# A two-block transformer on one core: routing, gate and memory-norm steps held in program order, bias rows repeated by transfers

## The chip, the cores and the metric

The kernel runs on one core of one Trainium2 chip. The metric is device time in microseconds (us), the median of repeated executions. Lower is better. The engines that matter here are TensorE (PE, matrix products), VectorE (DVE), ScalarE (ACT), GpSimd (POOL, here only an issuer of transfers) and SyncE (SP, the issuer of weight loads). Each takes its instructions strictly in the order in which they stand in its queue: one that waits holds up everything behind it on that engine.

## The reference, cut to what matters

256 tokens of width 2048 go through two blocks. The change touches the second half of the first block (`peer`) and the preparation of a bias for the second.

```python
def peer(h, wq, k1, k2, u, v):
    t = h.reshape(-1, d)                                # 256 x 2048
    q = (t @ wq).reshape(T, 8, 2, 128)
    s1 = jnp.einsum('thd,hnd->thn', q[:, :, 0], k1)     # 128 scores per head and half
    s2 = jnp.einsum('thd,hnd->thn', q[:, :, 1], k2)
    v1, i1 = lax.top_k(s1, 16)
    v2, i2 = lax.top_k(s2, 16)
    cand = v1[..., :, None] + v2[..., None, :]          # 16 x 16 candidates
    sc, pos = lax.top_k(cand, 16)                       # the 16 experts of a token and head
    g = jax.nn.softmax(sc, axis=-1)
    act = gelu(u[idx] @ t);  out = sum(g * act * v[idx])  # over 16384 experts
...
dist_bias = rel_bias[t5_bucket(jnp.arange(S))].T        # 8 heads, one bias per distance
m = rmsnorm_2(mem, g_mem)                               # needs the sums of squares of mem
```

## The kernel before

**The work.** Nearly all of it is dense matrix products in float32, each done as three products of a high and a low part: activations are split into `hTh` and `hTl`, and each block of weights into `whi` and `wlo`. The experts are not gathered: all 16384 rows of `u` are multiplied (`up`, eight groups of 2048 experts), the result is multiplied by a gate that is zero for experts not chosen (`gate`), and then by all rows of `v` (`down`, eight groups).

**The weight stream.** `load_w` brings 1 MB of weights into one of three `raw` buffers through SP's queue. `split_w` (two calls per `raw`) makes `whi` with a cast on ACT (line 114) and `wlo` with a subtraction on DVE (line 115, which needs `whi`). There are three buffers of each, so the two engines can be at most three splits ahead of PE. In `gemm_block` (down, and most projections) one split feeds 12 products of 512 columns (line 147), in `gemm_cols` (up) 24 products of 256 columns (lines 174 to 176).

**Side work.** Everything else is written as Python generators that are put in a queue (`later`). `step(rate)`, called after each 1 MB of weights, traces the next pieces of them, each up to its next `yield`. The rates stand in `RATES`: 1.5 pieces per MB in the last projection before `up` and in the first three groups of `up`, 0.6 in `down`, 1.7 in the third group of `down`. `drain()` traces what is left.

**The order.** The queue of an engine is not the order of tracing. A scheduler sorts the instructions of each engine by its own estimate of when their inputs are ready, and so it can move a traced instruction ahead of others on its engine if no data stand against it.

**The pieces that the change touches.**
- `route` (lines 799 to 838), 16 times: for one head and half of the tokens, the top 16 of two sets of 128 scores (`top16`), the sums of the pairs, the top 16 of those, the two indices (lines 818 to 829), then the softmax (an Exp on ACT at line 836). It is all on DVE except for small casts and the Exp on ACT. Five pieces each.
- `all_gates`: one-hot rows for 8 tokens at a time on DVE (`ohA`, `ohB`), products on PE, and the gates written to DRAM (`gd`).
- `gate(e)`: for each of four pieces, the activations and gates are fetched from DRAM into one of three `ag` buffers (`fetch`, POOL's queue), multiplied on DVE (line 955), cast to `hTh` on ACT (line 958) and subtracted to `hTl` on DVE (line 959). It prepares `down(e)` during `down(e-1)`, and `gate(0)` during the last group of `up`.
- `ahead`, during the third group of `down`: the memory (2 MB) is brought into two `raw` buffers of the weight stream and squared and summed on ACT (`sq_sum`, line 251, tile `ssm`); then one row of biases per head is computed by a matrix product (line 996), repeated on all 128 partitions, copied (line 998) and written to DRAM (`bd`), from where the second block reads it.

Of the kernel before, what the change touches and what calls it, by code (L numbers as in the profile page):

```python
# [9 lines left out]
F32 = mybir.dt.float32  # L10
# [3 lines left out]
AF = mybir.ActivationFunctionType  # L14
OP = mybir.AluOpType
# [4 lines left out]
P = 128  # L20
# [35 lines left out]
def build(tc, A, out):  # L56
    nc = tc.nc
    mm = nc.tensor.matmul

    es = ExitStack()  # L60
    with es:
# [40 lines left out]
        def drain():  # L102
            flush(-1)
            step(-1)

# [143 lines left out]
        def sq_sum(x, acc_col, n=512):  # L249
            junk = main.tile([P, 512], F16, name="junk", bufs=1)  # L250
            nc.scalar.activation(junk[:, :n], x, AF.Square, accum_out=acc_col)
# [10 lines left out]
        env = dict(locals())  # L262
# [485 lines left out]
def peer(env):  # L748
    z = NS(env)
    nc, ps, main, wp, A, tc, mm = z.nc, z.ps, z.main, z.wp, z.A, z.tc, z.mm  # L750
# [5 lines left out]
    with phase_pool(tc, "peer") as pp:  # L756
# [31 lines left out]
        def top16(src, vals, idx):  # L788
            n = src.shape[-1]
            tmp = scr[:, 3, 0:T]  # L790
            nc.vector.max(vals[:, 0:8], src)
# [5 lines left out]
        def route(h, t):  # L797
# [3 lines left out]
            for j in range(2):  # L801
# [5 lines left out]
            nc.vector.tensor_add(  # L807
                cd,
                v[:, 0].unsqueeze(2).to_broadcast([P, 16, 16]),
                v[:, 1].unsqueeze(1).to_broadcast([P, 16, 16]),  # L810
# [7 lines left out]
            nc.vector.tensor_scalar(ab[:, 0], pu, 4, None, OP.logical_shift_right)  # L818
# [16 lines left out]
            nc.vector.tensor_scalar_mul(mx, sc[:, 0:1], -1.0)  # L835
# [34 lines left out]
        def all_gates():  # L870
# [4 lines left out]
            for t0 in range(0, T, TG):  # L875
                gs = pp.tile([P, P, TG], F32, name="gs", bufs=3)
                for tb in range(0, TG, 8):
# [6 lines left out]
                    nc.vector.tensor_tensor(four(B2), io, row(i2T, t), OP.is_equal)  # L884
# [59 lines left out]
        def gate(e):  # L944
# [5 lines left out]
            for nb in range(4):  # L950
# [4 lines left out]
                nc.vector.tensor_mul(av, av, g.rearrange("p b c t -> p c b t"))  # L955
                yield
                cs = slice(nb * 4, nb * 4 + 4)
                nc.scalar.copy(wh[:, cs], a)  # L958
# [18 lines left out]
        def ahead():  # L977

            ssm = main.tile([P, 2, 4], F32, name="ssm", bufs=1)
            for t in range(2):  # L980
                mn = z.load_w(A["mem"][:, t].rearrange("p (a b) -> p a b", b=512))
                for b in range(4):
                    z.sq_sum(mn[:, b], ssm[:, t, b : b + 1])
                    yield
# [6 lines left out]
            nc.gpsimd.dma_start(bk, A["bucket"])  # L991
            env["bd"] = z.dram.tile([8, P, 384], F32, name="bd")
            yield
            for h in range(8):
                pb = z.mm_tile()
                mm(pb[:, :384], rb[:, h : h + 1].to_broadcast([33, P]), bk, start=True, stop=True)
                bv = pp.tile([P, 384], F32, name="bv", bufs=2)
                nc.scalar.copy(bv, pb[:, :384])
                nc.gpsimd.dma_start(env["bd"][h], bv)
                yield  # L1000
# [492 lines left out]
```

## Time and profile before

| | us |
|---|---|
| median of three executions | 3224.32 (3224.06 to 3224.76) |
| the profiled execution's own time | 3223.47 |
| its span, first to last instruction | 3221.7 |
| PE busy | 3183.3 |
| DVE busy | 2004.5 |
| ACT busy | 1529.6 |

The span is 1.8 us shorter than the time of the same execution. Busy is the time in which an engine had an instruction running; products follow each other in a pipeline, so a busy PE is one that was never left without work, not one at its peak.

### The profile page before, as it was taken

To read this page: it belongs to the slowest core of one execution; us is meant where nothing else is said; L and a number is where in the kernel's file an instruction comes from. 1 tells how busy PE (TensorE), PEld (TensorE's weight loads), DVE (VectorE), ACT (ScalarE), POOL (GpSimd) and SP (SyncE) were. 2 spreads that over 40 slices of the span, in tenths; PEclk is the share of its full clock that TensorE was granted. 3 is DMA by queue.
4 is the path that set the end of the run, shared out by engine and by line. 5 is a ranking of instruction groups with operands and counts; after the bars stand their busy time and mean duration, and the time that the engine had idled before them with its cause. 6 is when DMAs were issued, how large, how long until landed. Compare 5 with 4: busy or idle time off the path is not lost.

```text
span 3221.7 us, 45786 instructions
## 1 busy us (share of the span) xinstructions
PE 3183.3 (99%) x18818; PEld 2766.7 (86%) x18818; DVE 2004.5 (62%) x2812; ACT 1529.6 (47%) x1967; POOL 92.2 (3%) x126
## 2 busy tenths in 40 slices
PE   8999999999999999999999999999999999999998
PEld 7877788999999999777787778888888989899897
DVE  6665679955666654555555555799666555555555
ACT  6456555544444444444443444545656434444344
POOL 0000000000000010000100000000000000000000
PEclk9999999999999999999999999999999999999999
DMA  6544454565667786667666765555554555555554
GB/s 234 183 144 171 144 180 157 200 209 203 229 240 248 242 289 214 233 235 239 231 223 228 240 215 183 196 183 177 176 170 170 185 189 189 183 186 189 187 183 157
DMA packets 101475, 647.31 MB, mean 201 GB/s; under 512 B 11269, under 2 KB 12421, under 8 KB 32400
## 3 DMA queue, kind: packets, MB, share of 16 engines
q1 hardware_dynamic: 82512, 575.63, 51.7%
q0 software_dynamic: 18752, 68.74, 6.4%
q8 instruction: 147, 2.41, 0.3%
q14 instruction: 64, 0.52, 0.0%
HBM read 607.11 MB, written 37.22 MB: 200 GB/s over the span
## 4 chain that ended last, share of the span: by engine, by line
PE 72%; issue 15%; DVE 6%; DMA 4%; POOL 1%; ACT 1%; SPq 0%; ACTq 0%; POOLq 0%; DVEq 0%
PE acc L147 52%; PE acc L176 5%; PE acc L174 5%; PE acc L175 5%; DMA ag<-gd 3%; DVE wlo L115 2%; PE tp L214 1%; DVE scr L793 0%; POOL gd L898 0%; DVE i L828 0%; PE mm L743 0%; DVE hTl L959 0%; DMA raw<-in_peer_v_dram 0%; DMA raw<-in_mem_dram 0%; POOL act L915 0%
## 5 line engine op out<-in xcount | busy, mean ns | idle before, releaser
L115 DVE TENSOR_TENSOR wlo<-raw,whi 128x1024 fp32r<-128x1024 f32 x1064 | 1300.1, 1223 | 1041.8 <-ACT whi L114 1038.1
L114 ACT CAST whi<-raw 128x1024 fp32r<-128x1024 f32 x1064 | 1114.6, 1049 | 1455.2 <-PE acc L147 853.0
L147 PE MATMUL acc<-whi,hTh 128*128 128x512 f32 x2650 | 1061.7, 401 | 10.5 <-ACT whi L114 10.5
L147 PE MATMUL acc<-wlo,hTh 128*128 128x512 f32 x2650 | 1051.5, 397 | 7.0 <-DVE wlo L115 6.8
L147 PE MATMUL acc<-whi,hTl 128*128 128x512 f32 x2650 | 1050.8, 397 | 0.0
L176 PE MATMUL acc<-hTh,wlo 128*128 128x256 f32 x3072 | 866.8, 282 | 10.1 <-DVE wlo L115 9.9
L174 PE MATMUL acc<-hTh,whi 128*128 128x256 f32 x3072 | 868.0, 283 | 0.0
L175 PE MATMUL acc<-hTl,whi 128*128 128x256 f32 x3072 | 863.6, 281 | 0.0
L147 PEld LDWEIGHTS acc<-whi,hTh 128*128 128x128 f32 x2650 | 498.7, 188 | 132.7 <-ACT whi L114 10.9
L147 PEld LDWEIGHTS acc<-wlo,hTh 128*128 128x128 f32 x2650 | 499.0, 188 | 129.0 <-DVE wlo L115 13.2
L147 PEld LDWEIGHTS acc<-whi,hTl 128*128 128x128 f32 x2650 | 498.4, 188 | 120.7 <-issue 0.3
L176 PEld LDWEIGHTS acc<-hTh,wlo 128*128 128x128 f32 x3072 | 579.4, 189 | 14.9 <-DVE wlo L115 14.4
L174 PEld LDWEIGHTS acc<-hTh,whi 128*128 128x128 f32 x3072 | 579.8, 189 | 0.2
L175 PEld LDWEIGHTS acc<-hTl,whi 128*128 128x128 f32 x3072 | 579.7, 189 | 0.2
L1087 DVE SCALAR_TENSOR_TENSOR cc<-hc,vec,cc 128x256 f32<-128x256 f32 x240 | 102.1, 478 | 0.5
L955 DVE TENSOR_TENSOR ag<-ag 128x1024 f32<-128x1024 f32 x32 | 39.2, 1225 | 61.5 <-DMA ag<-gd 61.2
L958 ACT CAST hTh<-ag 128x1024 fp32r<-128x1024 f32 x32 | 32.9, 1050 | 31.7 <-DVE ag L955 22.5
L675 DVE TENSOR_TENSOR x<-acc,x 128x512 f32<-128x512 f32 x72 | 46.4, 681 | 0.3 <-PE acc L147 0.2
L911 DVE TENSOR_TENSOR at<-acc,rtok 128x512 f32<-128x512 f32 x64 | 43.7, 690 | 0.5
L959 DVE TENSOR_TENSOR hTl<-ag,hTh 128x1024 fp32r<-128x1024 f32 x32 | 38.5, 1222 | 1.6 <-ACT hTh L958 0.8
L915 POOL DMA_DIRECT2D act<-at x32 | 17.4, 545 | 741.4 <-ACT at L913 741.1
L940 POOL DMA_DIRECT2D ag<-gd x32 | 37.4, 1170 | 6.3 <-DMA gd<-gs 5.1
(314 smaller groups left out, 1496.3 us busy)
## 6 DMA issues: line engine op xcount, KB each, us to landing
raw<-in_peer_u_dram SPq DMA_DIRECT2D x128, 1024.0 KB, 4.9
raw<-in_peer_v_dram SPq DMA_DIRECT2D x128, 1024.0 KB, 4.9
raw<-in_w_dram SPq DMA_DIRECT2D x128, 1024.0 KB, 4.9
raw<-in_w_in_dram SPq DMA_DIRECT2D x83, 1024.0 KB, 4.9
raw<-in_w_out_dram SPq DMA_DIRECT2D x32, 1024.0 KB, 4.9
raw<-in_wq_dram SPq DMA_DIRECT2D x16, 1024.0 KB, 4.9
act<-at POOLq DMA_DIRECT2D x32, 512.0 KB, 4.3
gd<-gs POOLq DMA_DIRECT2D x16, 1024.0 KB, 5.6
```

What stands on the lines that cost most here:

```text
L114: nc.scalar.copy(hi[:, :kt, :n], raw[:, k0 : k0 + kt, :n])
L115: nc.vector.tensor_sub(lo[:, :kt, :n], raw[:, k0 : k0 + kt, :n], hi[:, :kt, :n].bitcast(F32))
L147: mm(o, a, b, start=start, stop=stop)
L174: mm(o, hi[:, k, cs], xh[:, kk], start=kk == 0 and c % 2 == 0, stop=False)
L175: mm(o, hi[:, k, cs], xl[:, kk], start=False, stop=False)
L176: mm(o, lo[:, k, cs], xh[:, kk], start=False, stop=kk == 15 and c % 2 == 1)
L675: nc.vector.tensor_add(x[:, t, sl], acc[t], x[:, t, sl])
L911: nc.vector.tensor_mul(at[:, 2 * c : 2 * c + 2], acc[c], rt)
L940: nc.gpsimd.dma_start(g, gd[e, :, :, nb * 4 : nb * 4 + 4])
L955: nc.vector.tensor_mul(av, av, g.rearrange("p b c t -> p c b t"))
L959: nc.vector.tensor_sub(wl[:, cs], a, wh[:, cs].bitcast(F32))
L1087: nc.vector.scalar_tensor_tensor(o, hc[:, c, tap : tap + T], w[:, tap : tap + 1], o, OP.mult, OP.add)
```

## The change

`pin` puts an instruction behind the last one that was traced before it on its own engine. It adds no wait at run time; it only takes from the scheduler the freedom to move that instruction forward. What depends on a pinned instruction moves with it. Pinned are: the first `max` of each `top16`, the sums of pairs, the first index step and the first softmax step in `route`; the first comparison of each group of 8 tokens in `all_gates`; the product (line 955) and the cast (line 958) in `gate`; each `sq_sum` of the memory in `ahead`, which is now also traced two pieces after its load; and the one product of the biases. That product makes all 8 heads at once, without repetition. Its 8 rows go to DRAM (`bd1`), are read back repeated on 128 partitions, four heads at a time (`br`, in the buffers of `at`), and are written to `bd`.

```diff
@@ -102,6 +102,9 @@
         def drain():
             flush(-1)
             step(-1)
+
+
+        pin = tc.keep_in_program_order
 
         def load_w(src, kt=4, n=512):
             raw = wp.tile([P, 4, 512], F32, name="raw", bufs=3)
@@ -248,7 +251,7 @@
 
         def sq_sum(x, acc_col, n=512):
             junk = main.tile([P, 512], F16, name="junk", bufs=1)
-            nc.scalar.activation(junk[:, :n], x, AF.Square, accum_out=acc_col)
+            return nc.scalar.activation(junk[:, :n], x, AF.Square, accum_out=acc_col)
 
 
         con = const.tile([P, NCON], F32)
@@ -788,7 +791,7 @@
         def top16(src, vals, idx):
             n = src.shape[-1]
             tmp = scr[:, 3, 0:T]
-            nc.vector.max(vals[:, 0:8], src)
+            z.pin(nc.vector.max(vals[:, 0:8], src))
             nc.vector.max_index(idx[:, 0:8], vals[:, 0:8], src)
             nc.vector.match_replace(tmp[:, :n], vals[:, 0:8], src, -3e38)
             nc.vector.max(vals[:, 8:16], tmp[:, :n])
@@ -804,10 +807,12 @@
             fi = rp.tile([P, 2, 16, 16], F16, name="if_p", bufs=1)
             nc.scalar.copy(fi, iu.unsqueeze(3).to_broadcast([P, 2, 16, 16]))
             cd = scr[:, 3, T : 2 * T].rearrange("p (a b) -> p a b", b=16)
-            nc.vector.tensor_add(
-                cd,
-                v[:, 0].unsqueeze(2).to_broadcast([P, 16, 16]),
-                v[:, 1].unsqueeze(1).to_broadcast([P, 16, 16]),
+            z.pin(
+                nc.vector.tensor_add(
+                    cd,
+                    v[:, 0].unsqueeze(2).to_broadcast([P, 16, 16]),
+                    v[:, 1].unsqueeze(1).to_broadcast([P, 16, 16]),
+                )
             )
             sc = rp.tile([P, 16], F32, name="sc_p", bufs=2)
             pu = rp.tile([P, 16], U32, name="pu_p", bufs=2)
@@ -815,7 +820,7 @@
             top16(cd.rearrange("p a b -> p (a b)"), sc, pu)
             yield
             ab = rp.tile([P, 2, 16], U32, name="ab_p", bufs=2)
-            nc.vector.tensor_scalar(ab[:, 0], pu, 4, None, OP.logical_shift_right)
+            z.pin(nc.vector.tensor_scalar(ab[:, 0], pu, 4, None, OP.logical_shift_right))
             nc.vector.tensor_scalar(ab[:, 1], pu, 15, None, OP.bitwise_and)
             abf = rp.tile([P, 2, 16], F16, name="abf_p", bufs=2)
             nc.scalar.copy(abf, ab)
@@ -832,7 +837,7 @@
 
             mx = rp.tile([P, 1], F32, name="mx_p", bufs=2)
             sm = rp.tile([P, 1], F32, name="sm_p", bufs=2)
-            nc.vector.tensor_scalar_mul(mx, sc[:, 0:1], -1.0)
+            z.pin(nc.vector.tensor_scalar_mul(mx, sc[:, 0:1], -1.0))
             nc.scalar.activation(sc, sc, AF.Exp, bias=mx, accum_out=sm)
             nc.vector.reciprocal(sm, sm)
             nc.scalar.mul(gsel[:, t, h * 16 : h * 16 + 16], sc, sm)
@@ -881,7 +886,7 @@
                     A1 = pp.tile([P, 8, P], F16, name="ohA", bufs=1)
                     B2 = pp.tile([P, 8, P], F16, name="ohB", bufs=2)
                     Ag = [pp.tile([P, 8, P], F16, name="ohA%d" % k, bufs=2) for k in range(2)]
-                    nc.vector.tensor_tensor(four(B2), io, row(i2T, t), OP.is_equal)
+                    z.pin(nc.vector.tensor_tensor(four(B2), io, row(i2T, t), OP.is_equal))
                     nc.vector.tensor_tensor(four(A1), io, row(i1T, t), OP.is_equal)
                     yield
                     for k, g in enumerate((gh, gl)):
@@ -952,10 +957,10 @@
                 a = ag[:, 0].rearrange("p (c t) -> p c t", c=4)
                 g = ag[:, 1].rearrange("p (b c t) -> p b c t", c=4, t=TG)
                 av = a.rearrange("p c (b t) -> p c b t", t=TG)
-                nc.vector.tensor_mul(av, av, g.rearrange("p b c t -> p c b t"))
+                z.pin(nc.vector.tensor_mul(av, av, g.rearrange("p b c t -> p c b t")))
                 yield
                 cs = slice(nb * 4, nb * 4 + 4)
-                nc.scalar.copy(wh[:, cs], a)
+                z.pin(nc.scalar.copy(wh[:, cs], a))
                 nc.vector.tensor_sub(wl[:, cs], a, wh[:, cs].bitcast(F32))
                 fetch()
                 yield
@@ -979,8 +984,10 @@
             ssm = main.tile([P, 2, 4], F32, name="ssm", bufs=1)
             for t in range(2):
                 mn = z.load_w(A["mem"][:, t].rearrange("p (a b) -> p a b", b=512))
+                yield
+                yield
                 for b in range(4):
-                    z.sq_sum(mn[:, b], ssm[:, t, b : b + 1])
+                    z.pin(z.sq_sum(mn[:, b], ssm[:, t, b : b + 1]))
                     yield
             env["rm"] = z.rstd_of(ssm, D, "rstdm")
 
@@ -989,14 +996,19 @@
             nc.vector.memset(rb[32:33], NEG)
             nc.gpsimd.dma_start(rb[0:32], A["rel_bias"])
             nc.gpsimd.dma_start(bk, A["bucket"])
+            bv = pp.tile([8, 384], F32)
+            yield
+            pb = z.mm_tile()
+            z.pin(mm(pb[:8, :384], rb, bk, start=True, stop=True))
+            nc.scalar.copy(bv, pb[:8, :384])
+            bd1 = z.dram.tile([8, 384], F32, name="bd1")
+            nc.gpsimd.dma_start(bd1, bv)
+
             env["bd"] = z.dram.tile([8, P, 384], F32, name="bd")
-            yield
-            for h in range(8):
-                pb = z.mm_tile()
-                mm(pb[:, :384], rb[:, h : h + 1].to_broadcast([33, P]), bk, start=True, stop=True)
-                bv = pp.tile([P, 384], F32, name="bv", bufs=2)
-                nc.scalar.copy(bv, pb[:, :384])
-                nc.gpsimd.dma_start(env["bd"][h], bv)
+            for h in range(0, 8, 4):
+                br = pp.tile([P, 4, 384], F32, name="br", tag="at", bufs=2)
+                nc.gpsimd.dma_start(br, bd1[h : h + 4].partition_broadcast(P))
+                nc.gpsimd.dma_start(env["bd"][h : h + 4].rearrange("h p j -> p h j"), br)
                 yield
 
         for nb in range(4):
```

The order on the engines moves as follows; `N` lines lower down in the changed file are the same lines (115 is now 118, 251 is 254, 955 is 960, 959 is 964, 114 is 117).

**DVE, in the routing, before.** Names: `wlo` is the weight stream, `v_p`, `iu_p`, `sc_p`, `pu_p`, `ab_p`, `eq_p` are the tiles of `route`.

```order
L115 TENSOR_TENSOR wlo<-raw,whi 128x1024
L818 TENSOR_SCALAR ab_p<-pu_p 128x16
L819 TENSOR_SCALAR ab_p<-pu_p 128x16
L793 MATCH_REPLACE scr<-v_p,scr 128x128
L791 MAX v_p<-scr 128x8
L794 MAX v_p<-scr 128x8
L837 RECIPROCAL sm_p<-sm_p 128x1
L792 MAX_INDEX iu_p<-v_p,scr 128x8
L795 MAX_INDEX iu_p<-v_p,scr 128x8
L791 MAX v_p<-scr 128x8
L793 MATCH_REPLACE scr<-v_p,scr 128x128
L115 TENSOR_TENSOR wlo<-raw,whi 128x1024
```

The same place in the changed kernel:

```order
L118 TENSOR_TENSOR wlo<-raw,whi 128x1024 x2
L823 TENSOR_SCALAR ab_p<-pu_p 128x16
L829 TENSOR_TENSOR eq_p<-abf_p,iok 128x512
L832 TENSOR_TENSOR eq_p<-eq_p,if_p 128x512
L833 TENSOR_REDUCE i_3350<-eq_p 128x2x16
L840 TENSOR_SCALAR mx_p<-sc_p 128x1
L118 TENSOR_TENSOR wlo<-raw,whi 128x1024
L842 RECIPROCAL sm_p<-sm_p 128x1
L794 MAX v_p<-scr 128x8
L795 MAX_INDEX iu_p<-v_p,scr 128x8
L796 MATCH_REPLACE scr<-v_p,scr 128x128
L797 MAX v_p<-scr 128x8
```

Before, ten steps that belong to more than one route stand between two subtractions of the weight stream, many of them beside one that they don't depend on. In the changed kernel one route runs at a time, its steps follow from each other, and there is at most one piece per subtraction. Counted over the whole queue, the 16 routes stand between the 134th and the 184th `wlo` before, and between the 134th and the 241st now. The loads of ACT's function tables for Exp (line 836) and Gelu (line 913), which take turns there, are 8 before and 22 now.

**DVE, at the start of the first group of `down`, before.** `ag` is a fetched piece, the L924 rows take the results of `down` into `x`.

```order
L115 TENSOR_TENSOR wlo<-raw,whi 128x1024 x2
L955 TENSOR_TENSOR ag<-ag 128x1024
L115 TENSOR_TENSOR wlo<-raw,whi 128x1024
L959 TENSOR_TENSOR hTl<-ag,hTh 128x1024
L115 TENSOR_TENSOR wlo<-raw,whi 128x1024
L955 TENSOR_TENSOR ag<-ag 128x1024
L115 TENSOR_TENSOR wlo<-raw,whi 128x1024 x2
L924 SCALAR_TENSOR_TENSOR x<-acc_13297,x 128x512
L924 SCALAR_TENSOR_TENSOR x<-acc_13298,x 128x512
L955 TENSOR_TENSOR ag<-ag 128x1024
L115 TENSOR_TENSOR wlo<-raw,whi 128x1024
L955 TENSOR_TENSOR ag<-ag 128x1024
```

The same place in the changed kernel:

```order
L118 TENSOR_TENSOR wlo<-raw,whi 128x1024 x2
L960 TENSOR_TENSOR ag<-ag 128x1024
L118 TENSOR_TENSOR wlo<-raw,whi 128x1024 x4
L964 TENSOR_TENSOR hTl<-ag,hTh 128x1024
L118 TENSOR_TENSOR wlo<-raw,whi 128x1024 x2
L929 SCALAR_TENSOR_TENSOR x<-acc_13297,x 128x512
L929 SCALAR_TENSOR_TENSOR x<-acc_13298,x 128x512
L118 TENSOR_TENSOR wlo<-raw,whi 128x1024 x2
L960 TENSOR_TENSOR ag<-ag 128x1024
L118 TENSOR_TENSOR wlo<-raw,whi 128x1024 x2
L964 TENSOR_TENSOR hTl<-ag,hTh 128x1024
```

Before, the four products of the next group stand within the first 9 splits of a group of 32; now they are 6 to 8 splits apart, and 2 apart in the third group, where the rate is higher. In the last group of `up` they stand at the splits 358 to 364 before (of the whole queue) and 380 to 392 now. The fetches on POOL are not pinned; each is issued when the `ag` buffer of three pieces earlier has been read (line 959), so all but the first three move with that line.

**ACT, around the sums of squares of the memory, before** (`raw` in the `ssm` rows is the memory's buffer):

```order
L114 CAST whi<-raw 128x1024 x4
L251 ACTIVATE junk,ssm<-raw 128x512 x2
L114 CAST whi<-raw 128x1024
L251 ACTIVATE junk,ssm<-raw 128x512 x2
L114 CAST whi<-raw 128x1024 x3
L251 ACTIVATE junk,ssm<-raw 128x512
L114 CAST whi<-raw 128x1024
L251 ACTIVATE junk,ssm<-raw 128x512 x2
L114 CAST whi<-raw 128x1024
L251 ACTIVATE junk,ssm<-raw 128x512
```

and in the changed kernel:

```order
L117 CAST whi<-raw 128x1024 x4
L254 ACTIVATE junk,ssm<-raw 128x512 x2
L117 CAST whi<-raw 128x1024 x2
L254 ACTIVATE junk,ssm<-raw 128x512
L117 CAST whi<-raw 128x1024 x2
L254 ACTIVATE junk,ssm<-raw 128x512
L117 CAST whi<-raw 128x1024 x2
L254 ACTIVATE junk,ssm<-raw 128x512
L117 CAST whi<-raw 128x1024 x2
L254 ACTIVATE junk,ssm<-raw 128x512 x2
```

The load of the first half of the memory stands at the same place of SP's queue. Before, ACT came to its first sum ahead of the two casts of the weights that were loaded just before it; now the sum stands behind these two and behind two more. The four sums of one half spread over four casts instead of one, and the memory holds one of the three `raw` buffers for that long. The weights that are loaded into that buffer next are those of the very next cast behind the last sum of the first half.

## Rows read from the trace of the kernel before

**Rows 1.** The page's part 1: busy time, share of the span, instructions.

```profile
PE 3183.3 (99%) x18818; PEld 2766.7 (86%) x18818; DVE 2004.5 (62%) x2812; ACT 1529.6 (47%) x1967; POOL 92.2 (3%) x126
```

**Rows 2.** Busy time by stretch: start:end, length, engines' busy us (instructions), granted clock, DMA.

```profile
490.00:640.00 150.00, 141.10 (x1031) 130.46 (x1030) 144.31 (x451) 82.07 (x136) 2.19 (x4) 1.00 0.51 176
...
1150.00:1180.00 30.00, 26.91 (x212) 26.09 (x211) 21.14 (x19) 13.40 (x15) 7.42 (x9) 0.96 1.02 333
1330.00:1340.00 10.00, 6.33 (x23) 4.71 (x22) 4.63 (x4) 2.10 (x2) 0.00 (x0) 0.90 0.54 169
1420.00:1430.00 10.00, 9.44 (x41) 7.19 (x40) 7.50 (x8) 4.19 (x4) 0.00 (x0) 1.00 0.76 264
1510.00:1530.00 20.00, 16.80 (x60) 12.74 (x59) 9.58 (x9) 7.25 (x14) 0.00 (x0) 0.83 0.73 248
```

**Rows 3.** The same view, DVE alone: line 115, line 911, line 828.

```profile
490.00:640.00 150.00, 56.82 (x47) 1.00 0.51 176
...
490.00:640.00 150.00, 5.19 (x8) 1.00 0.51 176
...
490.00:640.00 150.00, 15.22 (x13) 1.00 0.51 176
```

**Rows 4.** Busy time of a stretch of `up` without routing.

```profile
640.00:720.00 80.00, 80.00 (x678) 80.00 (x677) 39.27 (x36) 32.81 (x32) 1.60 (x3) 1.00 0.60 205
```

**Rows 5.** Timeline of DVE in the routing: start us, length us, instruction.

```profile
558.50 0.28 DVE L794 MAX8 v_p<-scr 128x8 f32<-128x128 f32 x1
558.69 0.28 DVE L791 MAX8 v_p<-scr 128x8 f32<-128x128 f32 x1
...
559.46 0.27 DVE L793 MATCH_REPLACE8 scr<-v_p,scr 128x128 f32<-128x128 f32 x1
559.77 0.29 DVE L794 MAX8 v_p<-scr 128x8 f32<-128x128 f32 x1
```

**Rows 6.** Timeline of ACT in the routing.

```profile
558.47 1.28 ACT L836 ACT_TABLE_LOAD   x1
559.76 0.31 ACT L836 ACTIVATE sc_p<-sc_p,mx_p 128x16 f32<-128x16 f32 x1
```

**Rows 7.** Groups of instructions: busy, mean ns | idle just before, what ended it.

```profile
L955 DVE TENSOR_TENSOR ag<-ag 128x1024 f32<-128x1024 f32 x32 | 39.2, 1225 | 61.5 <-DMA ag<-gd 61.2 <-DMA ag<-act 0.3
```

**Rows 8.** Timeline of DVE and PE, first group of `down`; in brackets the idle time before.

```profile
1335.19 1.22 DVE L955 TENSOR_TENSOR ag<-ag 128x1024 f32<-128x1024 f32 x1 [6.34 <-DMA ag<-gd]
...
1333.54 0.40 PE L147 MATMUL acc<-whi,hTh 128*128 128x512 f32 x1
1337.60 0.50 PE L147 MATMUL acc<-wlo,hTh 128*128 128x512 f32 x1 [3.67 <-DVE wlo L115]
...
1341.29 0.46 PE L147 MATMUL acc<-wlo,hTh 128*128 128x512 f32 x1
```

**Rows 9.** Timeline of PE, last group of `up`, after a wait of 2.16 us.

```profile
1177.60 0.41 PE L176 MATMUL acc<-hTh,wlo 128*128 128x256 f32 x1
...
1180.80 0.37 PE L176 MATMUL acc<-hTh,wlo 128*128 128x256 f32 x1
```

**Rows 10.** Timeline of ACT and PE, third group of `down`.

```profile
1516.70 0.63 ACT L251 ACTIVATE junk<-raw 128x512 f16<-128x512 f32 x1 [7.58 <-DMA raw<-in_mem_dram]
...
1519.16 0.80 PE L147 MATMUL acc<-whi,hTh 128*128 128x512 f32 x1 [2.73 <-ACT whi L114]
1520.42 0.80 PE L147 MATMUL acc<-wlo,hTh 128*128 128x512 f32 x1 [0.46 <-DVE wlo L115]
...
1525.71 0.41 PE L147 MATMUL acc<-wlo,hTh 128*128 128x512 f32 x1
```

**Rows 11.** The chain that ended last: start us, length us, what; bias products.

```profile
1563.09 1.48 PE mm L996 x4
```

**Rows 12.** Transfers: engine, count, size each, median us from issue to landing.

```profile
raw<-in_peer_v_dram SPq DMA_DIRECT2D x128, 1024.0 KB, 4.9
...
raw<-in_mem_dram SPq DMA_DIRECT2D x2, 1024.0 KB, 8.8
```

## The prediction

> **What bounds the kernel now.** I read the busy times first. PE is busy for 3183.3 of the 3221.7 us of the span [rows 1], so the only time to be had is what PE spends idle, what it spends at a low clock, and products that go away. Next I read the busy time in stretches of 10 us over the whole span and kept those in which PE is not fully busy; apart from the first loads and the last outputs, which the change doesn't touch, they lie in five places [rows 2]. At each I asked what PE waited for.
>
> 1. **Routing, 490 to 640 us.** PE is idle for 150 - 141.10 = 8.9 us while DVE is busy for 144.31 of 150 us [rows 2]. This is the only stretch of the five in which DVE is the bound. A little later, without routing, PE is busy throughout and DVE only half the time [rows 4].
> 2. **Last group of `up`, 1150 to 1180 us.** PE is idle for 30 - 26.91 = 3.1 us with DVE far from full [rows 2].
> 3. **First group of `down`, 1330 to 1340 us.** PE waits 3.67 us for a `wlo`. DVE had time for it, but it stood in its queue at a product of `gate`, waiting 6.34 us for a fetch, with the subtractions of the weight stream behind [rows 8]. Over the kernel DVE stands 61.2 us before such fetches in 32 products [rows 7]; most of it is covered by the splits made ahead.
> 4. **Second group, 1420 to 1430 us**: 0.56 us [rows 2].
> 5. **Third group, 1510 to 1530 us.** PE is idle for 20 - 16.80 = 3.2 us [rows 2]. ACT stood 7.58 us at a sum of squares whose memory had not landed, with the casts of the weight stream behind it [rows 10].
>
> The waits also cost clock. Over one dense stretch PE takes 80 / 678 = 0.118 us per product of 256 columns [rows 4], so about 0.236 us per 512. After the wait at 1337.6, nine products take 1341.29 - 1337.60 = 3.69 us [rows 8] instead of 2.12, so 1.6 us more; the granted clock of that stretch is 0.90 [rows 2], a mixture of the two levels 2.4 and 1.2 GHz. After the wait of 2.16 us in the last group of `up`, 15 products take 3.20 us [rows 9] instead of 1.77: 1.4 us. In the third group of `down`, 13 products take 1525.71 - 1519.16 = 6.55 us, 0.46 of it idle [rows 10], instead of 3.07: 3.0 us more.
>
> **The change part by part.**
>
> *Pinning of the routing.* The number of DVE instructions is the same; they are spread. Demand of one route: in 490 to 640 us DVE spends 144.31 on everything, 56.82 on 47 `wlo` and 5.19 on the results of `up`, and 13 of the 16 final reductions (line 828) fall there [rows 2, 3], so one route is (144.31 - 56.82 - 5.19) / 13 = 6.3 us. The 16 routes stand between 107 splits now, 6.7 splits each. For 6.7 splits PE needs 6.7 x 24 x 0.118 = 19.0 us [rows 4]. DVE needs 6.7 x 1.21 = 8.1 for the splits [rows 3], 6.3 for the route, and 1.1 for results of `up` (two of 0.65 us per 8 splits): 15.5 us. That leaves 3.5 us per route.
>
> Two costs come on top. Steps that follow from each other cannot overlap: a maximum that needs the step before it starts 559.77 - 559.46 = 0.31 us after it, one that doesn't 0.19 us [rows 5]. With 0.12 us for some 16 such pairs per route this is 0 (they stood so already) to 1.9 us. And DVE now waits for small steps of ACT: the cast of the indices and the Exp with its sum, from 0.3 us (another subtraction stands between) to some 1.8 us (a table load of 1.28 and an Exp of 0.31 [rows 6] in full). Together 0.3 to 3.7 us against 3.5 to spare. I take 2.3, nearer the middle since a subtraction of the weight stream often stands between. Then DVE is at 17.8 of 19.0 us, and the splits made ahead (three, 8.5 us of PE) carry single pieces. The stall goes, except for about 1.5 us where pieces cluster: 7.4 of 8.9 us saved. Bounds: 0 and 8.9.
>
> ACT gets 14 more table loads, 14 x 1.28 = 18 us [rows 6]. They lie beside PE's work: ACT is busy for 82.07 of 150 us even in the routing [rows 2]. If that cover were gone, they would cost up to 18 us.
>
> The Trainium skill speaks against this order. Its page "ScalarE: Activation LUTs", section "What ACT_TABLE_LOAD costs", says that each change to another set of tables costs the load and then a drain, 2.66 us in all, and advises to batch by set. The trace doesn't agree with the second half: the load starts at 558.47 and takes 1.28, and the Exp starts at 559.76 [rows 6]. By the page the 14 loads would be 37 us of ACT, by the row 18.
>
> *Pinning of `gate`.* In the last group of `up` the products move 22 to 28 splits back, over 60 us, so that their first fetches have long landed. In `down` they stand 6 to 8 splits (17 to 23 us) apart and each fetch is issued three pieces ahead. DVE then finds its input there and the subtractions are not held. What could be late next is `hTh`/`hTl` for the next group; the last piece stands at split 24 of 32, so 8 splits are left. I count all of places 2 to 4: 3.1 + 1.4, 3.67 + 1.6, 0.56, together 10.3 us. Bounds: 0 (the waits were for the transfers themselves) and 10.3.
>
> *Sums of the memory.* ACT comes to the first sum four casts later, 4 x 12 x 0.236 = 11 us, and a load of the memory takes 8.8 us [rows 12]; the wait of 7.58 us goes. What is late next: the first half holds a `raw` buffer until its fourth sum, and the next weights but none later must be loaded into it. From the start of the cast ahead of them it is 1.05 for the cast, 0.8 for the sum, 4.9 for the load [rows 12], then a cast and a subtraction, about 9 us, against three splits or 8.5 us of work that PE has. Here the fetches of `gate` are only 2 splits apart, so the load may take 8.8 as the memory's did: a stall of 0.5 to 4.5 us, the longer ones with clock. I take 2 us. Of 3.2 + 3.0 = 6.2 us, 4.2 are saved. Bounds: -3 and 6.2.
>
> *Biases.* Two passes of products take half of 1.48 / 2 us each: four records are 1.48 [rows 11], each of the 8 products is two records, so 0.74 us each. Seven of eight go, and PE is full there: 5.2 us. The bounds are the same, as PE has no other work to hide them. The new transfers (1.5 MB read back, the same 1.5 MB written) wait for each other on POOL's queue: three steps, each no longer than the 8.8 us of a 1 MB load in this crowded place [rows 12], 26 us at most. Behind them stands a fetch that is issued 7 splits or 20 us later, and its piece is wanted three pieces on. Cost: 0.
>
> **Sum.** 7.4 + 10.3 + 4.2 + 5.2 = 27.1 us, which takes the profiled execution from 3223.47 to 3196.4. The median of the runs is 0.85 us above that execution, so I predict 3197 us.
>
> **The rivals.**
> - *DVE stays full in the routing.* With both added costs at their upper end DVE needs 15.5 + 3.7 = 19.2 of 19.0 us, and clusters stall as before: nothing of 8.9 is saved. For it speak the narrow margin and 22 table loads; against it the stretch without routing, where DVE idles half the time. 3197 + 7.4 = 3204.
> - *The memory starves the weight stream.* The wait at the reload costs the 4.5 us above and a slow clock like the 3.0 us seen, and the second half something similar: 3 us are lost instead of 4.2 won. 3204.
> - *The change doesn't do what it says in `gate`.* The fetches are not pinned, DMA is at 1.02 of its capacity in 1150 to 1180 [rows 2], and the weights themselves may be late there. Then 10.3 us stay: 3207. Against it: in place 3 the wait is DVE's, at the fetch.
> - *Each change of tables holds ACT longer than the load*, as long again. This is a drain as the page "ScalarE: Activation LUTs" of the Trainium skill has it. With 1.28 us more per Exp, DVE needs 17.8 + 1.28 = 19.1 of 19.0 us: the 8.9 us stay and 0.1 x 16 come on top, 3206. Against it stand [rows 6], where Exp starts 0.01 us after the load.
> - *Slower.* DVE becomes the bound for all 107 splits. Everything else together saves 19.7 us and the old stall 8.9, so it takes 28.6 / 16 = 1.8 us more than 19.0 per route, 20.8 us, to lose the gain; for that the added costs would be 5.3 us per route instead of 2.3. If every one of the 16 dependent pairs and three ACT waits of 1.8 us came in full, 1.9 + 5.4 = 7.3, it would be 22.8 us and 16 x 3.8 - 28.6 = 32 us slower: 3256.
>
> **How the numbers follow.** The forecast has 0.60, DVE full 0.15, the memory 0.09, `gate` 0.06, the tables 0.03, slower 0.03; 0.04 are left for a gain that lies between these and none. The forecast's own range is 3193 (all bounds best, 30.6 us, give 3193.7) to 3202. The range of 3191 to 3208 takes in the next four cases one at a time. A difference of 0.2%, 6.4 us, is about what a measurement of this kernel can tell from no change; only the slower case and the mixed ones reach it. Faster 0.93, same 0.04, slower 0.03.
>
> **What would show it.** In the changed profile, 490 to 640 us should have PE above 148 us busy and DVE near 125, with routing until about 780 us. The group of the `gate` products should stand before fetches for a few us, not 61. PE at 1.00 clock through all of `down`, but for one short wait in its third group just behind the fourth sum of the memory. One bias product of two records. I am wrong if DVE is again above 95% of a stretch of 100 us in the routing, if the waits of PE in `down` have moved to ACT's casts waiting for weights, or if POOL's chain of biases holds back a fetch.

## The result, and the profile after

The changed kernel takes 3182.44 us (median of four runs, 3180.42 to 3184.12); the kernel before took 3224.19 us beside it. The ratio is 0.9871 with an interval of 0.9853 to 0.9888, a gain of 41.75 us. It is faster, as forecast, but by half as much again as the 27 us forecast, and 8.6 us below the lower end of the range.

The page's busy times of the changed kernel (busy, share of the span of 3179.9 us, instructions) answer to [rows 1]:

```profile
PE 3161.8 (99%) x18804; PEld 2759.0 (87%) x18804; DVE 2014.4 (63%) x2812; ACT 1548.6 (49%) x1974; POOL 91.1 (3%) x123
```

PE's idle time fell from 38.4 to 18.1 us and its busy time by 21.5 us. The five places of [rows 2], in busy time by stretch of the changed kernel (the last row is the one of the bias product):

```profile
490.00:640.00 150.00, 150.00 (x1164) 144.84 (x1164) 121.49 (x294) 86.53 (x116) 2.71 (x5) 1.00 0.56 194
1130.00:1160.00 30.00, 30.00 (x256) 30.00 (x255) 14.22 (x13) 12.40 (x12) 4.32 (x5) 1.00 0.85 286
1300.00:1320.00 20.00, 20.00 (x88) 16.05 (x87) 12.04 (x11) 8.59 (x9) 1.98 (x3) 1.00 0.78 265
1390.00:1420.00 30.00, 30.00 (x130) 24.13 (x129) 19.17 (x19) 13.15 (x13) 1.72 (x2) 1.00 0.67 230
1480.00:1520.00 40.00, 39.70 (x170) 31.59 (x169) 20.15 (x19) 19.28 (x28) 1.70 (x2) 1.00 0.81 279
1520.00:1580.00 60.00, 60.00 (x256) 47.46 (x256) 34.23 (x35) 27.25 (x31) 5.08 (x8) 1.00 0.74 266
```

PE is full in all of them but for 0.30 us, and the granted clock is 1.00. DVE is at 81% in the stretch where it was at 96%. One number should stop the reader: in the same 150 us of the routing PE had 1031 records before and has 1164 now, 133 more. The stretches don't hold quite the same work, but at 0.118 us each that is 15.7 us, where the idle time was 8.9.

To see where the 41.75 us lie, I numbered the 5792 products that read `wlo` and write `acc` in their order and compared the starts of equal numbers in the two traces. Between the places the difference holds to 0.03 us over hundreds of microseconds, so each step belongs to a place:

| products with `wlo` | place | gain by the traces, us | forecast, us |
|---|---|---|---|
| 0 to 540 | first loads | 1.2 | 0 |
| 570 to 900 | routing | 15.3 | 7.4 |
| 2250 to 2360 | last group of `up` | 6.0 | 4.5 |
| 2690 to 2780 | first group of `down` | 5.5 | 5.3 |
| 2800 to 2830 | second group | 0.9 | 0.6 |
| 2900 to 2960 | third group, memory | 6.4 | 4.2 |
| 2960 to 3040 | third group, biases | 5.6 | 5.2 |
| 3040 to the end | later groups, rest | 1.0 | 0 |

The first row is chance: in the traces of the ten experiments below, product 60 starts between 2.2 us later and 1.8 us earlier than before, and no edit touches what stands ahead of it.

### The profile page after: what moved, and what is told of

It is laid out like the page before. It is cut to its first block, busy times and chain, and to the rows that moved or that the text cites. A ratio compares the mean times of both kernels' runs of the same rounds, so it can differ in the third digit from the quotient of the medians.

```text
span 3179.9 us, 45745 instructions
## 1 busy us (share of the span) xinstructions
PE 3161.8 (99%) x18804; PEld 2759.0 (87%) x18804; DVE 2014.4 (63%) x2812; ACT 1548.6 (49%) x1974; POOL 91.1 (3%) x123
## 4 chain that ended last, share of the span: by engine, by line
PE 99%; ACT 0%; DMA 0%; DVE 0%; issue 0%; SPq 0%; ACTq 0%
PE acc L150 60%; PE acc L177 12%; PE acc L179 11%; PE acc L178 11%; PE tp L217 1%; PE mm L899 1%; PE mm L746 0%; PE mm L638 0%; PE tp L737 0%; PE mm L784 0%; PE mm L560 0%; PE mm L635 0%; PE mm L747 0%; PE mm L1187 0%; DMA raw<-in_peer_v_dram 0%; DMA raw<-in_w_in_dram 0%
## 5 line engine op out<-in xcount | busy, mean ns | idle before, releaser
L899 PE MATMUL mm<-ohA,ohB 128*128 128x128 f16 x512 | 35.9, 220 | 0.0
```

The source lines that it names most:

```text
L899: mm(pg[:, j], B2[:, tq + j], Ag[k][:, tq + j], start=k == 0, stop=k == 1)
```

## The experiments

Gains are given against the kernel before as it ran beside each experiment, since its median differed a little each time (3223.30, 3225.26 and 3225.61 us). The intervals of the ratios reach 0.0010 to 0.0017 to either side, that is 3 to 5 us; prices that differ by less are told apart by equal products in the traces, not by the medians. Each experiment is either the kernel before with one part of the change, or the changed kernel with one part taken out or something added. The small diffs show the lines that differ.

### One part alone, on the kernel before

**The routing pins alone (e1_route).** The four pins in `top16` and `route`.

```diff
-            nc.vector.max(vals[:, 0:8], src)
+            z.pin(nc.vector.max(vals[:, 0:8], src))
...
-            nc.vector.tensor_scalar_mul(mx, sc[:, 0:1], -1.0)
+            z.pin(nc.vector.tensor_scalar_mul(mx, sc[:, 0:1], -1.0))
```

> The kernel before with the four pins of the routing steps alone. Theory A (the gain of the whole change is larger than forecast because the idle time of PE in the routing, 8.9 us, leaves out a part of each stall: the starts of the products in that stretch are 14 to 15 us further apart than the regular spacing): 14 to 15 us faster, 3209 to 3210.5 us, with PE's idle time down by only about 9 us. Theory B (the idle time is the whole loss, and the unforeseen part of the gain comes from the other edits or from all of them together): 7 to 9 us faster, 3215 to 3217 us.

Measured: 3207.37 us against 3223.30, ratio 0.9952 (0.9935 to 0.9968), 15.9 us faster; 15.25 us of it between products 570 and 900. Theory A holds. Where do 15 us come from, if PE was idle for 9? Two stretches with nearly the same products show it, first of the kernel before, then of this run (busy time by stretch):

```profile
480.00:661.00 181.00, 172.10 (x1256) 159.67 (x1255) 164.08 (x499) 95.59 (x153) 2.72 (x5) 1.00 0.52 180
```

```profile
480.00:645.00 165.00, 165.00 (x1249) 157.81 (x1249) 133.12 (x326) 93.72 (x127) 2.73 (x5) 1.00 0.55 191
```

The 7 records that differ are 0.8 us, so the same products take 165.8 us instead of 181.0, 15.2 less, of which only 8.9 stood as idle time. The missing part is seen in the timeline of PE in the kernel before (start, length, in brackets the idle time before):

```profile
546.90 0.28 PE L175 MATMUL acc<-hTl,whi 128*128 128x256 f32 x1
548.23 0.39 PE L176 MATMUL acc<-hTh,wlo 128*128 128x256 f32 x1 [1.05 <-DVE wlo L115]
548.45 0.28 PE L174 MATMUL acc<-hTh,whi 128*128 128x256 f32 x1
548.57 0.28 PE L175 MATMUL acc<-hTl,whi 128*128 128x256 f32 x1
...
601.90 0.28 PE L174 MATMUL acc<-hTh,whi 128*128 128x256 f32 x1
602.01 0.28 PE L175 MATMUL acc<-hTl,whi 128*128 128x256 f32 x1
602.28 0.39 PE L176 MATMUL acc<-hTh,wlo 128*128 128x256 f32 x1
602.51 0.28 PE L174 MATMUL acc<-hTh,whi 128*128 128x256 f32 x1
```

Records are 0.28 us long but start every 0.12 us, so each is drawn 0.16 us into the time of the next. The wait that is shown as 1.05 us kept the product 548.23 - 546.90 - 0.12 = 1.21 us from its regular start, and the one behind it came 0.22 instead of 0.12 us later. At 602.28 there is a wait too, 0.27 instead of 0.12 us, and 0.23 behind it; the trace calls none of it idle. Over 490 to 641 us, 18 starts have idle time ahead of them, 8.9 us; by the spacing of the starts these cost 11.8 us, the products right behind them 1.9, and 24 late starts without any idle time 2.4. That makes 16.1 us, of which 1.0 remain in this run.

**Gate's pins alone (e2_gate).** The pins of gate's product on DVE and of its cast on ACT.

```diff
-                nc.vector.tensor_mul(av, av, g.rearrange("p b c t -> p c b t"))
+                z.pin(nc.vector.tensor_mul(av, av, g.rearrange("p b c t -> p c b t")))
...
-                nc.scalar.copy(wh[:, cs], a)
+                z.pin(nc.scalar.copy(wh[:, cs], a))
```

> The kernel before with the two pins of gate's product and cast alone. Theory A (each stall costs what the starts of the products show: 6.0 us in the last group of up, 5.4 in the first group of down, 0.8 in the second, 1.2 in later ones): 13 us faster, 3211 us, with the third group of down still waiting for the memory. Theory B (as forecast, idle time and clock): 10.3 us faster, 3214 us.

Measured: 3206.18 against 3223.30, ratio 0.9947 (0.9931 to 0.9964), 17.1 us faster, more than either theory. The places of gate give what A says (6.0, 5.5 and 0.9 us by equal products). What A had wrong is the third group: it waits far less for the memory, though its sums stand as before. Group of gate's products (busy, mean ns, idle before) and ACT at the first sum of each half:

```profile
L957 DVE TENSOR_TENSOR ag<-ag 128x1024 f32<-128x1024 f32 x32 | 39.0, 1218 | 0.0
```

```profile
1501.40 0.63 ACT L253 ACTIVATE junk<-raw 128x512 f16<-128x512 f32 x1 [1.33 <-DMA raw<-in_mem_dram]
...
1516.84 0.63 ACT L253 ACTIVATE junk<-raw 128x512 f16<-128x512 f32 x1 [1.86 <-DMA raw<-in_mem_dram]
```

All 61 us of DVE's waits [rows 7] are gone, and ACT's first wait for the memory is 1.33 us, where [rows 10] have 7.58. In the kernel before, gate issued four of its fetch pairs from 1490.86 to 1502.48, just ahead of the memory at 1505.62; here they are 5.6 us or more apart from 1485.01 on, and the first half of the memory was issued at 1494.81. From its issue to ACT's first sum that half took 11.1 us before and takes 6.6 here; for the second half it is 6.7 us before and 9.4 here. That the crowding made the difference is read from these times; no run moves the fetches and nothing else. By equal products the place of the first half (2900 to 2960) gains all its 6.4 us without any pin of its own, and 1.3 are lost again in 2960 to 3040, where PE waits behind the second half: 5.1 us together.

**The memory's pins alone (e3_mem).** Two steps of delay and the pinned sums, in `ahead`.

```diff
+                yield
+                yield
                 for b in range(4):
-                    z.sq_sum(mn[:, b], ssm[:, t, b : b + 1])
+                    z.pin(z.sq_sum(mn[:, b], ssm[:, t, b : b + 1]))
```

> The kernel before with the sums of squares of the memory pinned two steps later, alone. Theory A (the wait goes as a whole and the reload of the raw buffer stalls nothing): 6.2 us faster, 3218 us. Theory C (as forecast, 2 us are lost again at the reload): 4.2 us faster, 3220 us. Theory D (gate's unpinned products meet the reload): no change or up to 3 us slower.

Measured: 3222.59 against 3223.30, ratio 0.9998 (0.9988 to 1.0008), no difference. In the trace products 2900 to 2960 gain 5.2 us, so the wait does go; but products 3040 to 3080 lose 5.5, behind unpinned products of gate that now meet other loads. DVE's row there waits for a fetch and holds the subtractions up:

```profile
1611.11 1.28 DVE L926 SCALAR_TENSOR_TENSOR x<-acc,x 128x512 f32<-128x512 f32 x2
1617.85 1.23 DVE L957 TENSOR_TENSOR ag<-ag 128x1024 f32<-128x1024 f32 x1 [5.46 <-DMA ag<-gd]
```

Theory D comes nearest: a wait in one place was passed on to the next. The last group of `up` too, which this edit doesn't touch, lost 9.8 us here, 8.8 in the next run and 6.5 in e1_route, against 6.0 in the trace before: what unpinned fetches cost differs by execution, and the ten runs spread over 5.6 us.

**The biases alone (e4_bias).** The whole second half of `ahead` as in the change.

```diff
-            for h in range(8):
-                pb = z.mm_tile()
-                mm(pb[:, :384], rb[:, h : h + 1].to_broadcast([33, P]), bk, start=True, stop=True)
...
+            z.pin(mm(pb[:8, :384], rb, bk, start=True, stop=True))
...
+                nc.gpsimd.dma_start(br, bd1[h : h + 4].partition_broadcast(P))
```

> The kernel before with the bias rows made by one product and repeated by transfers, alone. Theory A (seven products of 0.74 us go and nothing waits for the new transfers): 5.2 us faster, 3219 us, no new wait in the third group of down. Theory B (the transfers hold back gate's fetches on POOL's queue): less than 3 us faster or slower, with longer waits of DVE for fetched pieces behind them.

Measured: 3219.30 against 3223.30, ratio 0.9987 (0.9977 to 0.9996), 4.0 us faster, with a spread of 10 us between runs, again with unpinned fetches. Of the gain, 6.2 us lie between products 2960 and 3040, the place of the biases. DVE's waits for fetched pieces are 65.6 us, 61.5 before, but the next fetch on POOL is released by DVE's `hTl` 16.9 us behind the chain, so the chain held no fetch back on POOL's queue. It agrees with A, but the medians don't fix the size.

**The pin in `all_gates` alone (e6_gates).**

```diff
-                    nc.vector.tensor_tensor(four(B2), io, row(i2T, t), OP.is_equal)
+                    z.pin(nc.vector.tensor_tensor(four(B2), io, row(i2T, t), OP.is_equal))
```

> The kernel before with the pin in all_gates alone. PE has no stall where the gates are built (800 to 1150 us), so both theories expect no change: 3223 us, give or take 1. If the end of the gates sets when gate's first fetches can start, the stall in the last group of up changes: 2 to 6 us either way.

Measured: 3224.28 against 3225.26, ratio 0.9996 (0.9986 to 1.0006), no difference, as expected. In its trace the last group of `up` lost 8.4 us, within the 6.0 to 9.8 of the other kernels without gate's pins.

### The changed kernel with one part taken out

Without the stalls of gate, kernels spread less, so these give the better prices. The edits are those above, undone.

**Without the memory's pins (e5_nomem).**

```diff
-                yield
-                yield
                 for b in range(4):
-                    z.pin(z.sq_sum(mn[:, b], ssm[:, t, b : b + 1]))
+                    z.sq_sum(mn[:, b], ssm[:, t, b : b + 1])
```

> The changed kernel without the pins and the two steps of delay at the sums of squares of the memory. Theory A (gate's pins alone already take away most of the wait for the memory, since its fetches no longer crowd around the load): about 1.4 us slower than the changed kernel, 3184 us, with 0.5 to 1 us of idle PE near 1500. Theory B (as forecast, the memory's own pins save 4.2 us or more): 3186.6 to 3189 us.

Measured: 3184.96 against 3225.26, 40.3 us faster than before (ratio 0.9871, 0.9855 to 0.9888), 1.4 us less than the whole change. The medians can't tell that from B's 4.2, but the traces do: by equal products it is 0.9 us less, all of it between 2960 and 3040, and the 6.4 us of 2900 to 2960 are there in full. Theory A.

**Without the new bias rows (e9_nobias).**

```diff
-            z.pin(mm(pb[:8, :384], rb, bk, start=True, stop=True))
...
+            for h in range(8):
+                pb = z.mm_tile()
+                mm(pb[:, :384], rb[:, h : h + 1].to_broadcast([33, P]), bk, start=True, stop=True)
```

> The changed kernel with the eight bias products and their copies as before. Theory A (each of seven products costs 0.74 us of a PE that has nothing else to do): 5.2 us slower than the changed kernel, 3187.6 us. Theory E (they also cost clock, as in the run with the memory's pins alone, where eight records of bias products within 3.4 us were followed by nine products 0.43 us apart instead of 0.236 though PE was never idle): up to 1.7 us more, 3189 us.

Measured: 3190.20 against 3225.61 (ratio 0.9891, 0.9875 to 0.9906), 35.4 us faster than before, so the biases are worth 6.3 us in the medians. The two profiled executions differ by 3186.94 - 3181.70 = 5.2 us, A's value, at full clock, although eight records of bias products stand within 3.4 us here too. In the executions without a trace the mean granted clock is 0.998 here (0.999 in the traced one) and 0.998 to 0.999 in the changed kernel (1.000), so some time at a lower clock is in both medians; where it lies, and whether the other 1.1 us are that (E), isn't shown.

**Without the routing pins (e10_noroute).**

```diff
-            z.pin(nc.vector.max(vals[:, 0:8], src))
+            nc.vector.max(vals[:, 0:8], src)
...
```

> The changed kernel without the four pins of the routing steps. Theory A (the stalls of the routing cost what the starts of the products show): 14 to 15 us slower than the changed kernel, 3197 us, with PE idle for about 9 us in 490 to 640. Theory B (they cost the idle time): 9 us slower, 3191 us. If the gain of the routing pins depends on the other edits, it differs from the 15.9 us of these pins alone by more than 2 us.

Measured: 3198.71 against 3225.61 (ratio 0.9916, 0.9902 to 0.9929), 26.9 us faster than before, so the pins are worth 14.9 us here and 15.9 alone, by equal products 15.3 both times: the routing doesn't depend on the other edits. The stretch of [rows 2] is back, with 8.9 us of idle time for 14.9 us of loss:

```profile
490.00:640.00 150.00, 141.07 (x1027) 130.24 (x1026) 144.84 (x453) 82.09 (x135) 2.19 (x4) 1.00 0.51 175
```

### More work for DVE in each route

Four sums in every route in e7_dve1, eight in e8_dve2, behind each `top16` and behind the final reduction. They only add time to DVE.

```diff
             nc.vector.max_index(idx[:, 8:16], vals[:, 8:16], tmp[:, :n])
+            z.pin(nc.vector.tensor_tensor(dmy, x[:, 0, 0:512], x[:, 1, 0:512], OP.add))
```

> The changed kernel with four added DVE sums of 128x512 in every route (about 0.68 us each, 2.7 us per route; what they write is read by nobody). Theory A (DVE is busy for 84 to 87% of the stretches from 510 to 790 us, so 2.5 to 3 us of every 19.0 are to spare, and the waits inside a route cost nothing): 0 to 5 us slower than the changed kernel, 3182 to 3187 us. Theory B (as forecast, 17.8 of 19.0 us per route are taken): 1.5 us x 16 = 24 us, less the 8.5 us that the splits ahead cover, 15 us slower: 3197 us.

> The same with eight sums in every route (5.4 us per route, what the rival Slower needs). Theory A: 5.4 - 2.7 = 2.7 us over, x 16 = 43, less 8.5: 35 us slower than the changed kernel, 3217 us; PE's idle time rises by clearly less than the time does, as each wait hides about 0.27 us (the record of the product ahead of it ends 0.16 us after a following one could start, and the next one comes 0.1 us late). Theory B: 4.2 us over x 16, less 8.5: 59 us slower, 3241 us; idle time rises as much as the time.

Measured: 3183.60 against 3225.26 with four, 41.7 us faster than before (ratio 0.9867, 0.9851 to 0.9884), so four sums more per route cost nothing in the medians, and 0.5 us in the trace. With eight, 3199.78 (ratio 0.9919, 0.9902 to 0.9936), 25.5 us faster than before: 16.3 us of the gain are lost. A had the loss at eight (35 us) more than twice too high. The same 2665 records in the changed kernel and with eight sums:

```profile
480.00:810.00 330.00, 330.00 (x2665) 322.92 (x2664) 272.12 (x634) 186.08 (x239) 7.36 (x13) 1.00 0.59 204
```

```profile
480.00:827.00 347.00, 335.49 (x2665) 325.46 (x2664) 333.18 (x760) 187.48 (x243) 7.38 (x13) 1.00 0.56 194
```

DVE's records overlap too: a sum's record is 0.68 us long, but DVE's busy time grows by 333.18 - 272.12 = 61.1 us for 760 - 634 = 126 more instructions, 0.48 us each. So eight sums are 3.9 us of DVE per route and not 5.4, four about 2.0 and not 2.7. Counted so, with 8.5 us covered by the splits ahead, A's room of 2.7 us per route gives a loss of 11 us at eight and B's room of 1.2 one of 35; the 16.3 measured lie nearer A.

The same products take 17 us longer, and PE's idle time is 347 - 335.49 = 11.5 us of it. A short stretch at a lower clock (0.66 in 690 to 695 us, behind a wait of 1.85 us) accounts for 1.5 us, as 17 products follow each other at 0.21 instead of 0.12 us there. The remaining 4 us, about a quarter of the price, are not in the idle time, as with the stalls of the kernel before.

## Why the prediction was wrong

**The step that failed** is the first sentence on what bounds the kernel, that "the only time to be had is what PE spends idle, what it spends at a low clock, and products that go away", and with it the term "7.4 of 8.9 us saved" and its upper bound of 8.9. A late start that is shorter than the overhang of the record ahead isn't in the idle time at all, and a longer one is in it with 0.16 us too little. In a stretch with some forty short waits (e1_route) this is 6 us of 15. The spacing of starts, which I used to price the low clock, would have shown it here too, with the products of 256 and of 512 columns taken apart. The term should have been 15; with it alone the sum is 34.7 us and the forecast 3189.6.

The Trainium skill has the reason on its page "Perfetto Trace Analysis", section "Tensor Engine Instruction (MATMUL, LD_WEIGHTS)": the end of a TensorE record is computed from the instruction's size and an access delay, "a model, not a measurement". The trace agrees in so far as its records of 0.28 us start 0.12 us apart and overlap; that their ends are computed no row shows.

**The added costs of the routing** (2.3 us per route of 3.5 to spare) were too high as well. With four sums, 2.0 us, added to each route almost nothing is lost (e7_dve1); as the splits made ahead may cover another 8.5 / 16 = 0.5 us per route, the costs were at most 3.5 - 2.0 + 0.5 = 2.0. With eight, 3.9 us (e8_dve2), the 16.3 us lost and the 8.5 covered are 1.5 us per route, so the costs were about 1.5 + 3.5 - 3.9 = 1.1, an estimate that takes the 3.5 as they stand. This error wasn't in the sum; it gave the first rival and the slower one odds that were too high. DVE's 121.49 us in 490 to 640 (forecast near 125) and the last Exp of the routing at 767.7 us (780) agree with the plan of one piece per subtraction. The table loads are 11 and 11, as counted, and lie beside PE's work (groups of ACT, the last one the Exp behind the first loads: busy, mean ns, idle before):

```profile
L841 ACT ACT_TABLE_LOAD x11 | 14.1, 1283 | 0.2
L918 ACT ACT_TABLE_LOAD x11 | 14.1, 1283 | 0.2
L841 ACT ACTIVATE sc_p<-sc_p,mx_p 128x16 f32<-128x16 f32 x16 | 4.9, 308 | 4.1 <-DVE mx_p L840 3.8
```

The rule of the Trainium skill, page "ScalarE: Activation LUTs", section "What ACT_TABLE_LOAD costs", that each change of tables also costs a drain, is still not borne out: [rows 6] have the Exp 0.01 us behind the load, and in the changed kernel ACT stands idle ahead of all 16 Exps for 4.1 us together, 3.8 of them for DVE's `mx_p`. Its advice to batch by set, which the page gives in its section "Table sets: the hidden batching unit", speaks against an order that gained 15 us: ACT was not what PE waited for.

**Gate** was right in its mechanism and low in size, 10.3 where its three places gave 12.3: the same hidden part, with fewer and longer waits. The three places give the same 6.0, 5.5 and 0.9 us in every trace with gate's pins; no run takes these pins alone out. All 32 products now find their input (kernel after, the group of [rows 7]):

```profile
L960 DVE TENSOR_TENSOR ag<-ag 128x1024 f32<-128x1024 f32 x32 | 38.9, 1215 | 0.0
```

**The memory** was credited to the wrong edit. Of 4.2 us that I gave to the delay of the sums, 0.9 to 1.4 are its own, at the second half; the 6.4 of the place itself come with gate's pins alone (e2_gate, e5_nomem), whose fetches no longer crowd the first load. As I had added the places and not the edits, the sum didn't suffer by this. What it did suffer by is the 2 us at the reload. That wait came where I put it, behind the fourth sum, but 0.30 us long (0.57 by the starts). Timeline of ACT, then of PE, in the changed kernel:

```profile
1502.66 0.63 ACT L254 ACTIVATE junk<-raw 128x512 f16<-128x512 f32 x1
1503.19 0.19 ACT L254 ACTIVATION_READ_ACCUMULATOR junk<-raw 128x1 f32 x1
1508.49 2.00 ACT L117 CAST whi<-raw 128x1024 fp32r<-128x1024 f32 x2 [5.11 <-DMA raw<-in_peer_v_dram]
```

```profile
1510.85 0.51 PE L150 MATMUL acc<-wlo,hTh 128*128 128x512 f32 x1 [0.30 <-DVE wlo L118]
```

From the sum to the next cast it is 1508.49 - 1503.38 = 5.1 us, so the load took about the 4.9 us of the weights and not the 8.8 that I feared.

**The biases** came out as worked out: one product of two records, 0.81 us at 1532.98, and 5.2 to 6.3 us gained. The chain on POOL's queue runs from 1534.80 to its last issue, and the next fetch of gate is only issued at 1562.95 (timeline of POOL; in brackets the idle time):

```profile
1534.80 0.51 POOL L1005 DMA_DIRECT2D bd<-bv  x1 [48.85 <-ACT bv L1003]
1537.84 1.06 POOL L1010 DMA_DIRECT2D br<-bd  x2 [2.53 <-DMA bd<-bv]
1542.66 0.77 POOL L1011 DMA_DIRECT2D bd<-br  x1 [3.77 <-DMA br<-bd]
1546.76 0.77 POOL L1011 DMA_DIRECT2D bd<-br  x1 [3.33 <-DMA br<-bd]
1562.95 0.55 POOL L943 DMA_DIRECT2D ag<-act  x1 [15.42 <-DVE hTl L964]
```

The last idle time is ended by DVE's row, not by the chain, so nothing stood behind it.

**The rivals.** None came. The one that ended slower put its turning point at 5.3 us of added costs per route, 3.0 more than forecast; with 3.9 us more the kernel was still 25.5 us faster than before.

**In sum**: 7.9 us of the 14.7 that the forecast lacks are the routing, 2.0 gate, 2.2 the memory's place, 0.4 the biases, 1.0 later waits that I had not priced, and 1.2 the chance of the first loads.

## What to carry to other kernels

On an engine whose records overlap, price a stall by the spacing of starts, or by the time that the same count of instructions takes in an undisturbed stretch; idle time is a lower bound, and the worse the shorter and more frequent the waits are. Where an in-order engine feeds the bound one, one small step per fed piece is worth more than a favourable order of the steps among themselves. And credit a gain to an edit only after a run with that edit alone and one with all but that edit: a wait at a crowded place may belong to what crowds it.

## What the runs showed of the hardware

In e3_mem the granted clock fell while PE was busy throughout (5.00 of 5.00 us in the slices from 1585 to 1595, granted clock 0.83 in both, that is, partly at the lower level of 1.2 GHz). Ahead of it stood eight records of bias products, which use 33 of 128 rows, from 1584.05 to 1588.21. Timeline of PE:

```profile
1584.05 2.43 PE L1000 MATMUL mm<-bk,rb 33*128 33x384 f32 x6
1586.41 0.50 PE L149 MATMUL acc<-whi,hTh 128*128 128x512 f32 x1
...
1587.30 0.91 PE L1000 MATMUL mm<-bk,rb 33*128 33x384 f32 x2
1588.14 0.66 PE L149 MATMUL acc<-whi,hTh 128*128 128x512 f32 x1
1588.60 0.63 PE L149 MATMUL acc<-wlo,hTh 128*128 128x512 f32 x1
1589.03 0.63 PE L149 MATMUL acc<-whi,hTl 128*128 128x512 f32 x1
```

The products behind start 0.43 us apart instead of 0.23. In e9_nobias eight of the same records stand as close, four from 1552.89 and four from 1554.80 us with one other product between, PE is as busy, and the granted clock stays at 1.00:

```profile
1552.89 1.55 PE L1000 MATMUL mm<-bk,rb 33*128 33x384 f32 x4
1554.37 0.50 PE L149 MATMUL acc<-whi,hTh 128*128 128x512 f32 x1
1554.80 1.55 PE L1000 MATMUL mm<-bk,rb 33*128 33x384 f32 x4
1556.29 0.50 PE L149 MATMUL acc<-wlo,hTh 128*128 128x512 f32 x1
1556.62 0.39 PE L149 MATMUL acc<-whi,hTl 128*128 128x512 f32 x1
1556.85 0.39 PE L149 MATMUL acc<-whi,hTh 128*128 128x512 f32 x1
```

So such products alone don't bring the clock down each time; what did in e3_mem stays open.

Product 60 of those with `wlo` starts between 60.86 and 64.88 us in the twelve traces, and from there to product 540 the distance between any trace and the one of before changes by at most 0.15 us. So 4 us of the spread between executions arise in the first loads.
